# Differential scores of 128 rows, raw weight tiles by phase, and row sums behind the eighth up product

## The chip, the cores and the metric

The kernel runs on one core of a Trainium2 chip. The metric is the device time of one execution in microseconds (us). The engines are named as in the profile: PE is TensorE (PEld its weight loads), DVE is VectorE, ACT is ScalarE, POOL is GpSimd, and SP is SyncE, whose queue issues the DMAs. L12 is line 12 of the kernel.

## The reference

Two layers of a diffusion transformer block work on 512 tokens of 1024 channels: 256 latent tokens and 256 context tokens. In layer 1 only the latent tokens need an output. Cut to what matters here:

```
mod  = silu(c) @ w_mod[i] + b_mod[i]           # six vectors a layer; silu(c_ctx) for the context
h    = rms_norm(x) * (1 + mod[1]) + mod[0]
p    = split(h @ w_in[i])                      # q, k, v of four token mixers
# differential attention: 4 heads, 2 halves of 32 channels each
q, k = rope(rms_norm(q)), rope(rms_norm(k))    # context: no rope
sc   = (q @ k.T) / sqrt(32)                    # 8 score matrices
a    = softmax(sc[half 0]) - lam * softmax(sc[half 1])
yb   = a @ v
# neighbourhood (na), grouped (gq) and latent (ml) attention likewise
x    = x + mod[2] * (sum_i sigmoid(h @ w_gate[i]) * (y_i @ w_branch[i])) @ w_out
h2   = rms_norm(x) * (1 + mod[4]) + mod[3]
u    = conv3(h2 @ w_up)                        # 5632 channels, three taps along the tokens
x    = x + mod[5] * (silu(u_gate) * u_val) @ w_down
```

## The kernel before, in words

**Products.** Both factors of every large product are split into a high part, which TensorE's fp32r format holds, and the low rest, and three products are added up (hi hi, lo hi, hi lo): mm3, lines 277 to 280. Weights come in tiles of 128 x 1024 (512 KB). For each, wload (line 267) issues the DMA into a raw tile on SP's queue, ScalarE casts it to the high part wh (line 272), and VectorE subtracts to get the low part wl (line 257, in lo_of). The pools wraw, whi and wlo have four buffers each. Products accumulate in PSUM, in three buffers called acc; attention scores have two, sc, and transposes two, tp.

**Order.** The kernel is written with generators, drive() interleaves them by weights, and the framework's scheduler then fixes the order of each engine's queue. Each engine works its queue off in that order and waits by semaphores.

**Row sums.** The products with w_mod have a single row of input, so they are done on VectorE. mods (line 329) loads a raw tile of w_mod (line 339) and multiplies it, once for the latent and once for the context vector, with cact, silu of the conditioning laid out over all partitions, and sums along the row into one column of M (line 349). There are 128 such sums; 48 stand in the attention of layer 0 and its last merge, and the last 56 tiles of the plan (80 sums) are driven beside the MLP of layer 0 (line 1143) with four raw tiles of their own, the pool mr. cact (1 MB) is loaded near the start (line 945) and put through Silu on ScalarE (line 946).

**Differential scores.** use_qk normalizes and rotates queries and keys; to_ST (line 591) transposes them on TensorE (line 607) and takes the high and low parts from PSUM. head_scores (line 756) makes a score matrix of 128 queries and 512 keys (256 for the context's queries): one matmul of 64 rows (line 767: the high part against both parts of the other side) and one of 32 rows (line 768). In layer 1 neighbourhood and grouped attention are split like this too, with 64 channels: 128 rows and 64 rows.

**The MLP.** After the output projection (split_tail, line 1008, whose last three parts are worked off half by half so that the norm's sums of squares ss end early), each chunk of 128 channels is modulated (operations t and hl on VectorE, hh on ScalarE). ffn (line 1115) makes the first four up products of layer 0 in two halves of 256 tokens each, which are eight products of the generator, and from there 512 tokens at a time. conv (line 1066) puts the three taps onto each product: one operation on ScalarE, two on VectorE (u, lines 1075 and 1076), which free the acc buffer. Behind the 20th up product comes the first group of down products, down(0), which adds to xt. An up product of 512 tokens is 24 matmuls.

**The start of layer 1.** The loop at line 922 modulates a chunk for both halves of the tokens and multiplies it with the weights for keys and values of neighbourhood attention into four PSUM tiles kv, two for the latent and two for the context tokens (lines 929 to 932).

## Time and profile before

| what | us |
|---|---|
| time, median of 3 runs (lowest, highest) | 1481.22 (1481.22, 1482.71) |
| the profiled execution's own time | 1481.19 |
| its span, first to last instruction | 1479.4 |
| busy: PE / DVE / ACT / POOL | 1428.8 / 1054.5 / 667.5 / 204.3 |
| mean granted clock of TensorE | 0.989 |

The profile is of one execution. Busy times of an engine are those in which it works on an instruction; shares are of the span. A matmul's end is modelled, so the pace of TensorE is read from the distance between the starts of two matmuls and not from their durations, which overlap. "x4" behind a row joins four equal instructions. A releaser behind "<-" is the work whose end let a waiting instruction go.

### The profile page before, as it was taken

The page shows a single profiled execution, that of the slowest core. Times are in us where ns is not written, and L with a number is a line of the kernel's source. Part 1 is how long each engine was busy: PE and PEld are TensorE (multiplying, and loading weights), DVE is VectorE, ACT ScalarE, POOL GpSimd, SP SyncE. Part 2 cuts the span into 40 slices and gives each one's busy share as a digit, 9 for nine tenths or more (in the row PEclk, how much of TensorE's full clock was granted, in tenths as well). Part 3 has the DMA queues.
Part 4 walks back from the last instruction along what each step waited for, and adds up shares of the span by engine and source line. Part 5 has one row for each costly group of instructions (what it writes and reads, how often), then busy time and mean ns, then how long its engine had stood idle before and what let it go on. Part 6 is the DMA issues. An engine that isn't in the chain of part 4 may idle for free.

```text
span 1479.4 us, 22328 instructions
## 1 busy us (share of the span) xinstructions
PE 1428.8 (97%) x8526; PEld 1197.5 (81%) x8526; DVE 1054.5 (71%) x1911; ACT 667.5 (45%) x1197; POOL 204.3 (14%) x191
## 2 busy tenths in 40 slices
PE   6999999999999997999999999899999999899999
PEld 3787777776777887888888888798788889799999
DVE  5688676658776589999856553668777575787884
ACT  5445544444333333444134432356646544564662
POOL 0343001213111200000000000034122331000000
PEclk9999999999999998999999999999999999999999
DMA  9532122214234364568822322333232344455553
GB/s 377 189 103 77 45 88 68 83 53 133 86 114 165 135 218 152 193 221 272 282 94 92 99 93 79 107 101 121 72 104 93 115 140 132 132 182 184 180 179 113
DMA packets 57931, 202.19 MB, mean 137 GB/s; under 512 B 6561, under 2 KB 8097, under 8 KB 57185
## 3 DMA queue, kind: packets, MB, share of 16 engines
q1 hardware_dynamic: 57824, 200.77, 40.2%
q8 instruction: 67, 1.10, 0.3%
q14 instruction: 40, 0.32, 0.1%
HBM read 199.69 MB, written 1.05 MB: 136 GB/s over the span
## 4 chain that ended last, share of the span: by engine, by line
PE 88%; DVE 6%; issue 3%; ACT 2%; DMA 1%; POOL 0%; SPq 0%; POOLq 0%; DVEq 0%; ACTq 0%
PE acc L278 24%; PE acc L280 24%; PE acc L279 24%; PE av L834 3%; PE sc L753 3%; PE tp L826 2%; DVE junk L349 2%; PE sc L768 2%; PE sc L767 1%; DVE wl L257 1%; ACT wh L272 1%; DVE t L254 1%; DMA raw<-in_wb_dram 1%; DMA mraw<-in_wb_dram 1%; PE acc L729 1%
## 5 line engine op out<-in xcount | busy, mean ns | idle before, releaser
L272 ACT CAST wh<-raw 128x1024 fp32r<-128x1024 f32 (+1 forms) x272 | 279.8, 1029 | 438.2 <-PE acc L279 336.6
L257 DVE TENSOR_TENSOR wl<-raw,wh 128x1024 fp32r<-128x1024 f32 (+1 forms) x272 | 331.4, 1218 | 158.7 <-ACT wh L272 156.3
L278 PE MATMUL acc<-hh,wh 128*128 128x256 f32 (+1 forms) x1248 | 424.7, 342 | 15.8 <-DVE u L254 8.7
L279 PE MATMUL acc<-hl,wh 128*128 128x256 f32 (+1 forms) x1248 | 419.4, 337 | 0.8 <-DVE hl L254 0.8
L280 PE MATMUL acc<-hh,wl 128*128 128x256 f32 (+1 forms) x1248 | 420.1, 337 | 0.0
L278 PEld LDWEIGHTS acc<-hh,wh 128*128 128x128 f32 x1248 | 239.8, 193 | 44.5 <-issue 12.9
L279 PEld LDWEIGHTS acc<-hl,wh 128*128 128x128 f32 x1248 | 240.6, 193 | 26.6 <-issue 3.3
L280 PEld LDWEIGHTS acc<-hh,wl 128*128 128x128 f32 x1248 | 240.5, 193 | 26.5 <-issue 4.3
L257 POOL TENSOR_TENSOR r<-v,mhalf 128x4 f32<-128x4 f32 (+3 forms) x59 | 81.6, 1387 | 736.5 <-DVE v L404 461.8
L349 DVE SCALAR_TENSOR_TENSOR junk<-raw,cact 128x1024 bf16<-128x1024 f32 x128 | 156.8, 1225 | 21.7 <-DMA raw<-in_wb_dram 21.1
L278 PE MATMUL acc<-wh,hh 128*128 128x256 f32 (+3 forms) x496 | 148.8, 300 | 4.2 <-ACT hh L423 4.2
L279 PE MATMUL acc<-wl,hh 128*128 128x256 f32 (+3 forms) x496 | 147.5, 297 | 0.0
L280 PE MATMUL acc<-wh,hl 128*128 128x256 f32 (+3 forms) x496 | 145.1, 298 | 0.1
L279 PE MATMUL acc<-al,wh 128*128 128x256 f32 (+1 forms) x370 | 121.5, 328 | 0.0
L278 PE MATMUL acc<-ah,wh 128*128 128x256 f32 (+1 forms) x370 | 121.5, 328 | 0.0
L280 PE MATMUL acc<-ah,wl 128*128 128x256 f32 (+1 forms) x370 | 121.4, 328 | 0.0
L254 DVE SCALAR_TENSOR_TENSOR u<-acc,smt,u 128x255 f32<-128x255 f32 (+1 forms) x184 | 108.4, 593 | 1.5
L278 PEld LDWEIGHTS acc<-wh,hh 128*128 128x128 f32 x496 | 94.9, 191 | 14.1 <-ACT hh L423 7.1
L776 ACT ACTIVATE p<-sc,nm 128x512 f32<-128x512 f32 (+1 forms) x120 | 74.1, 618 | 66.0 <-DVE nm L773 37.9
L280 PEld LDWEIGHTS acc<-wh,hl 128*128 128x128 f32 x496 | 94.5, 191 | 9.4 <-issue 5.5
L279 PEld LDWEIGHTS acc<-wl,hh 128*128 128x128 f32 x496 | 95.0, 191 | 6.8 <-issue 4.6
L773 DVE TENSOR_REDUCE nm<-sc 128x1 f32<-128x512 f32 (+1 forms) x120 | 71.1, 597 | 35.4 <-PE sc L768 24.8
(165 smaller groups left out, 2067.7 us busy)
## 6 DMA issues: line engine op xcount, KB each, us to landing
raw<-in_wb_dram SPq DMA_DIRECT2D x328, 512.0 KB, 3.4
mraw<-in_wb_dram SPq DMA_DIRECT2D x16, 512.0 KB, 10.2
raw<-in_wb_dram SPq DMA_DIRECT2D x20, 384.0 KB, 2.9
x<-in_xT_dram SPq DMA_DIRECT2D x2, 1024.0 KB, 6.3
bt<-in_bias_dram SPq DMA_DIRECT2D x8, 256.0 KB, 3.2
xt<-in_xT_dram SPq DMA_DIRECT2D x2, 1024.0 KB, 7.1
raw<-in_wb_dram SPq DMA_DIRECT2D x4, 320.0 KB, 2.8
cact<-in_cb_dram SPq DMA_DIRECT2D x1, 1024.0 KB, 11.4
```

The source lines that it names most:

```text
L254: V.scalar_tensor_tensor(out=out, in0=in0, scalar=scalar, in1=in1, op0=op0, op1=op1)
L257: e.tensor_tensor(out=out, in0=a, in1=b, op=op)
L272: A.copy(h[:, :w], r[:, :w])
L278: mm(ps, lhsT=a[0], rhs=b[0], start=first, stop=False)
L279: mm(ps, lhsT=a[0], rhs=b[1], start=False, stop=False)
L280: mm(ps, lhsT=a[1], rhs=b[0], start=False, stop=last)
L349: V.scalar_tensor_tensor(out=junk, in0=r, scalar=1.0, in1=cact[:, st_], op0=ALU.mult, op1=ALU.mult, accum_out=o)
L753: mm(sps[:, :n], lhsT=q[o:o + d, c:c + P], rhs=k[o:o + d, T - n:], start=True, stop=True)
L768: mm(sps[:, :n], lhsT=q[r1, 4 + i, c:c + P], rhs=kk[r1], start=False, stop=True)
L773: V.tensor_reduce(out=nm, in_=sps[:, :n], op=ALU.max, axis=AX.X, negate=True)
L776: A.activation(out=p[:, :n], in_=sps[:, :n], func=AF.Exp, bias=nm, accum_out=s)
L834: mm(av[64 * j:64 * j + 64], lhsT=V_[:, 4 - nk + i, vcol(hd):vcol(hd) + 64], rhs=PTs[j][:, i], start=i == 0, stop=i == nk - 1, tile_positi ...
```

## The change

Five things are changed.

1. Raw weight tiles by phase: wraw has three buffers instead of four, and wraw_load takes its tile from a list of pools in turn. In the attention of layer 0 the list holds wraw alone. From the last merge of layer 0 to the end of its MLP, weights use wraw1 (four buffers), and the row sums use wraw; the pool mr is gone. In layer 1 the list is three times wraw and once wraw2 (one buffer).
2. cact moves into a pool that is opened only once the first layer's input tile is closed; its load and its Silu stand at the same place in the code, but wait for that space. The row sums' unused product goes into a temporary tile instead of the tile junk.
3. Differential queries and keys: to_D copies the high parts (ScalarE) and subtracts the low ones (VectorE) into a staging tile before the transposes, laid out so that each head's half fills 128 rows: hi, hi, lo, lo on one side and hi, lo, hi, lo on the other. One step later TensorE transposes it in four pieces and one operation brings it out of PSUM, on VectorE or ScalarE in turn. A score is then one matmul of 128 rows. The context's rows get their gain in a further multiplication on VectorE. The weight of this chain in drive goes from 12 + nq to 20 + nq.
4. The row sums beside the MLP are issued behind the last tap of the eighth product (tc.issue_after).
5. In layer 1 the loop at the start modulates the latent half of every chunk and serves the two latent kv tiles first, and then the context half with the other two.

```diff
-    wraw = pool("wraw", 4)
+    wraw = pool("wraw", 3)
...
+    cyc = [[wraw], 0]
+
     def wraw_load(l, key, n=1024):
-        r = wraw.tile([P, 1024], F32, name="raw")
+        cyc[1] += 1
+        r = cyc[0][cyc[1] % len(cyc[0])].tile([P, 1024], F32, name="raw")
         nc.sync.dma_start(out=r[:, :n], in_=wb[l, KIDX[key], :, :n])
...
-    cact = const.tile([P, 2, D], F32, name="cact")
-    junk = const.tile([P, D], mybir.dt.bfloat16, name="junk")
...
-                V.scalar_tensor_tensor(out=junk, in0=r, scalar=1.0, in1=cact[:, st_], op0=ALU.mult,
-                                       op1=ALU.mult, accum_out=o)
+                with tc.issue_after(behind) if behind is not None else nullcontext():
+                    V.scalar_tensor_tensor(out=tmp.tile([P, D], mybir.dt.bfloat16, name="t"), in0=r, scalar=1.0, in1=cact[:, st_], op0=ALU.mult,
+                                           op1=ALU.mult, accum_out=o)
...
+        def to_D(dst, src, i, isq):
...
+            def parts_():
+                w4 = stage().rearrange("p a n -> p (a n)").bitcast(F32R)
+                w = w4.rearrange("p (g x y d) -> p g x y d", g=4, x=2, y=2)
+                s = src.rearrange("p (g d) -> p g d", g=4).unsqueeze(2).to_broadcast([P, 4, 2, 32])
+                hi, lo = (w[:, :, 0], w[:, :, 1]) if isq else (w[:, :, :, 0], w[:, :, :, 1])
+                A.copy(hi, s)
+                tt(V, lo, s, hi.bitcast(F32), ALU.subtract)
+                got.append(w4.bitcast(F32))
+
+            def turn():
+                tp = tp_p.tile([P, 4, P], F32, name="tp")
+                for g in range(4):
+                    nc.tensor.transpose(tp[:, g], got[0][:, g * P:(g + 1) * P], ident)
+                evac(A if i else V, dst, tp)
+
+            return [parts_, turn]
...
+                elif key == "df":
+                    tt(V, v4(st, h), v4(st, h), dgt[:, tab].unsqueeze(1).unsqueeze(1).to_broadcast([P, na, h, d]), ALU.mult)
...
+                    fs = [to_D(z[:, 4 * i:4 * i + 4, a * P:(a + 1) * P], st[:, a, i * P:(i + 1) * P], i, dst is qT)
+                          for a in range(na) for i in range(2)]
...
+            if d == 32:
+                mm(sps[:, :n], lhsT=q[:, 4 * i + r, c:c + P], rhs=k[:, 4 * ik + r, T - n:], start=True, stop=True)
+                return sps, n
...
             for bc, p_ in zip(bcs, FULL):
-                modulate(xt, bc, s1, M, 0, c, p_)
+                if l == 0 or p_[2] == 0:
+                    modulate(xt, bc, s1, M, 0, c, p_)
...
+            for t in range(4) if l == 0 else range(2):
+                kv_mm(c, t)
+        if l:
+            for c in range(KD):
+                modulate(xt, bcs[1], s1, M, 0, c, FULL[1])
+                for t in range(2, 4):
+                    kv_mm(c, t)
...
+            ces = ExitStack()
+            cact = spool(ces, "cact", 1, side="right").tile([P, 2, D], F32, name="cact")
             nc.sync.dma_start(out=cact, in_=cb)
...
-                     win_block(l, "dq", qh, use_qk(qT, "df", 8, 32, *q32, vec("dgq"), 0, 1)), flush()), 12 + nq),
+                     win_block(l, "dq", qh, use_qk(qT, "df", 8, 32, *q32, vec("dgq"), 0, 1)), flush()), 20 + nq),
...
+            wes = ExitStack()
+            cyc[0] = [spool(wes, "wraw1", 4)]
...
-            stt(u3[:, :, 0:255], p3[:, :, 1:256], cw[:, 2:3], u3[:, :, 0:255], ALU.mult, ALU.add)
+            tap = stt(u3[:, :, 0:255], p3[:, :, 1:256], cw[:, 2:3], u3[:, :, 0:255], ALU.mult, ALU.add)
+            behind.append(tap.ins)
...
-            mrp = spool(fes, "mr", 4)
-            drive((body, 70), (mods(56, mrp, 2), 59))
+            with_order = mods(56, wraw, 2, behind[-1])
+            drive((body, 70), (with_order, 59))
...
+            cyc[0] = [wraw, wraw, wraw, ctx.enter_context(tc.tile_pool(name="wraw2", bufs=1))]
```

The order of VectorE's queue at the beginning of the MLP of layer 0, before, where the first chunks are modulated (t and hl); "junk,M<-raw,cact" is a row sum:

```order
L257 TENSOR_TENSOR wl<-raw,wh 128x1024
L254 SCALAR_TENSOR_TENSOR t<-xt,s_5389,sc 128x256 x2
L257 TENSOR_TENSOR ss<-ss,t 128x256
L349 SCALAR_TENSOR_TENSOR junk,M<-raw,cact 128x1024
L254 SCALAR_TENSOR_TENSOR hl<-t,M,hh 128x256
L254 SCALAR_TENSOR_TENSOR t<-xt,s_5389,sc 128x256
L254 SCALAR_TENSOR_TENSOR hl<-t,M,hh 128x256
L349 SCALAR_TENSOR_TENSOR junk,M<-raw,cact 128x1024
L404 TENSOR_SCALAR v<-tp 128x2
L254 SCALAR_TENSOR_TENSOR t<-xt,s_5389,sc 128x256 x2
```

The same place in the changed kernel:

```order
L257 TENSOR_TENSOR wl<-raw,wh 128x1024
L254 SCALAR_TENSOR_TENSOR t<-xt,s_5498,sc 128x256 x2
L257 TENSOR_TENSOR ss<-ss,t 128x256
L254 SCALAR_TENSOR_TENSOR hl<-t,M,hh 128x256
L254 SCALAR_TENSOR_TENSOR t<-xt,s_5498,sc 128x256
L254 SCALAR_TENSOR_TENSOR hl<-t,M,hh 128x256
L254 SCALAR_TENSOR_TENSOR t<-xt,s_5498,sc 128x256 x2
L254 SCALAR_TENSOR_TENSOR hl<-t,M,hh 128x256
L406 TENSOR_SCALAR v<-tp 128x2
L254 SCALAR_TENSOR_TENSOR hl<-t,M,hh 128x256
```

The row sums have left this part of the queue; from the first update of xt by the output projection to the eighth product's last tap there is none.

VectorE's queue among the up products of 512 tokens, before (u_...<-acc is a tap, wl the low part of a weight, al the low part of the activations):

```order
L257 TENSOR_TENSOR wl<-raw,wh 128x1024
L254 SCALAR_TENSOR_TENSOR u_5763<-acc,smt,u_5763 128x2x255
L349 SCALAR_TENSOR_TENSOR junk,M<-raw,cact 128x1024
L257 TENSOR_TENSOR al<-u_5572,ah 128x512
L254 SCALAR_TENSOR_TENSOR u_5763<-acc,smt,u_5763 128x2x255
L349 SCALAR_TENSOR_TENSOR junk,M<-raw,cact 128x1024
L257 TENSOR_TENSOR wl<-raw,wh 128x1024
L254 SCALAR_TENSOR_TENSOR u_5806<-acc,smt,u_5806 128x2x255
L349 SCALAR_TENSOR_TENSOR junk,M<-raw,cact 128x1024
L254 SCALAR_TENSOR_TENSOR u_5806<-acc,smt,u_5806 128x2x255
```

The changed kernel, directly behind the tap that ends the eighth product:

```order
L254 SCALAR_TENSOR_TENSOR u_5710<-acc,smt,u_5710 128x255 x2
L351 SCALAR_TENSOR_TENSOR t,M<-raw,cact 128x1024 x3
L257 TENSOR_TENSOR u_5681<-u_5681,u_5710 128x512
L351 SCALAR_TENSOR_TENSOR t,M<-raw,cact 128x1024 x2
L257 TENSOR_TENSOR wl<-raw,wh 128x1024
L254 SCALAR_TENSOR_TENSOR u_5869<-acc,smt,u_5869 128x2x255
L351 SCALAR_TENSOR_TENSOR t,M<-raw,cact 128x1024
L257 TENSOR_TENSOR al<-u_5681,ah 128x512
L351 SCALAR_TENSOR_TENSOR t,M<-raw,cact 128x1024 x2
L257 TENSOR_TENSOR wl<-raw,wh 128x1024
L254 SCALAR_TENSOR_TENSOR u_5869<-acc,smt,u_5869 128x2x255
L254 SCALAR_TENSOR_TENSOR u_5914<-acc,smt,u_5914 128x2x255
```

The sums stand there in threes. Counted over VectorE's queue, 72 of them lie between that tap and the last update of xt by down(0), and the other eight stand before the start of layer 1.

TensorE's queue at two differential scores of layer 0, before (L834 and L826 are products with the values and transposes of probabilities of an earlier score):

```order
L767 MATMUL sc<-kS,qS 128x512
L768 MATMUL sc<-kS,qS 128x512
L834 MATMUL av<-PT,Vt 64x256 x3
L826 MATMUL tp<-C,p 128x128 x4
L767 MATMUL sc<-kS,qS 128x512
L768 MATMUL sc<-kS,qS 128x512
```

The changed kernel (L646 is the transpose in to_D, L866 that of probabilities):

```order
L802 MATMUL sc<-kB,qB 128x512
L646 MATMUL tp<-C,st 128x128 x4
L866 MATMUL tp<-C,p 128x128 x2
L646 MATMUL tp<-C,st 128x128 x4
L802 MATMUL sc<-kB,qB 128x512
L646 MATMUL tp<-C,st 128x128 x4
```

Where two matmuls of part of the rows made a score, one stands now, and groups of four transposes have come in between.

## Rows read from the trace of the kernel before

**Rows 1.** The page, busy time by engine (us, share of the span, instructions) and the chain that ended last, by engine.

```profile
PE 1428.8 (97%) x8526; PEld 1197.5 (81%) x8526; DVE 1054.5 (71%) x1911; ACT 667.5 (45%) x1197; POOL 204.3 (14%) x191
...
PE 88%; DVE 6%; issue 3%; ACT 2%; DMA 1%; POOL 0%; SPq 0%; POOLq 0%; DVEq 0%; ACTq 0%
```

**Rows 2.** The table of stretches: from and to, length, busy us (and instructions) of PE, PEld, DVE, ACT and POOL, granted clock of TensorE, mean busy share of the DMA engines, GB/s.

```profile
20.00:40.00 20.00, 18.16 (x123) 11.53 (x123) 14.86 (x40) 13.09 (x21) 0.00 (x0) 1.00 1.02 411
60.00:260.00 200.00, 200.00 (x1147) 153.23 (x1146) 146.05 (x304) 97.46 (x209) 53.47 (x39) 1.00 0.24 76
520.00:608.00 88.00, 74.70 (x468) 69.30 (x467) 82.33 (x158) 32.14 (x55) 3.55 (x3) 0.92 0.57 191
960.00:1060.00 100.00, 99.62 (x671) 85.81 (x671) 76.98 (x142) 63.12 (x119) 34.70 (x26) 1.00 0.29 98
```

**Rows 3.** What TensorE waited for from 520 to 608 us: operation and line, releaser, us in total, times, longest.

```profile
PE acc L278 <- DVE u L254: 8.7, 2, 5.9
PE acc L278 <- ACT hh L423: 3.9, 1, 3.9
```

**Rows 4.** The timeline of TensorE from 588 to 596 us: start, duration, instruction; in brackets the idle time before it and its releaser.

```profile
588.91 0.55 PE L278 MATMUL acc<-hh,wh 128*128 128x256 f32 x1 [5.94 <-DVE u L254]
...
589.47 0.41 PE L280 MATMUL acc<-hh,wl 128*128 128x256 f32 x1
589.68 0.41 PE L278 MATMUL acc<-hh,wh 128*128 128x256 f32 x1
...
594.53 0.28 PE L280 MATMUL acc<-hh,wl 128*128 128x256 f32 x1
594.64 0.28 PE L278 MATMUL acc<-hh,wh 128*128 128x256 f32 x1
```

**Rows 5.** The timeline of VectorE from 596 to 601 us (same columns): two row sums with an operation between them, and a third directly behind the second.

```profile
596.83 1.22 DVE L349 SCALAR_TENSOR_TENSOR junk<-raw,cact 128x1024 bf16<-128x1024 f32 x1
...
597.98 0.48 DVE L254 SCALAR_TENSOR_TENSOR u<-acc,smt,u 128x255 f32<-128x255 f32 x1
598.37 1.21 DVE L349 SCALAR_TENSOR_TENSOR junk<-raw,cact 128x1024 bf16<-128x1024 f32 x1
...
599.63 1.23 DVE L349 SCALAR_TENSOR_TENSOR junk<-raw,cact 128x1024 bf16<-128x1024 f32 x1
```

**Rows 6.** The timeline of TensorE around 153 us: a differential score with 512 columns, and the matmuls behind it.

```profile
153.37 0.50 PE L767 MATMUL sc<-kS,qS 64*128 64x512 f32 x1
153.80 0.49 PE L768 MATMUL sc<-kS,qS 32*128 32x512 f32 x1
154.22 0.50 PE L279 MATMUL acc<-hl,wh 128*128 128x512 f32 x1
154.56 0.39 PE L280 MATMUL acc<-hh,wl 128*128 128x512 f32 x1
154.79 0.40 PE L278 MATMUL acc<-hh,wh 128*128 128x512 f32 x1
```

**Rows 7.** The same around 173 us: a differential score with 256 columns.

```profile
173.66 0.28 PE L280 MATMUL acc<-wh,hl 128*128 128x256 f32 x1
173.87 0.38 PE L767 MATMUL sc<-kS,qS 64*128 64x256 f32 x1
174.18 0.38 PE L768 MATMUL sc<-kS,qS 32*128 32x256 f32 x1
174.49 0.50 PE L278 MATMUL acc<-hh,wh 128*128 128x512 f32 x1
174.83 0.39 PE L279 MATMUL acc<-hl,wh 128*128 128x512 f32 x1
```

**Rows 8.** The same around 1001 us: the first matmuls of two scores of layer 1 that use all 128 rows (x2), and the one behind them.

```profile
1000.99 0.63 PE L767 MATMUL sc<-kS,qS 128*128 128x512 f32 x2
1001.46 0.28 PE L280 MATMUL acc<-wh,hl 128*128 128x256 f32 x1
```

**Rows 9.** Groups of TensorE's instructions by line and shape: rows of the array, output and type, count, busy us, mean ns of one, idle time before them. The second matmul of a score (L768, 32 rows) has the same counts as the first (L767, 64 rows).

```profile
L767 PE MATMUL sc<-kS,qS 64*128 64x512 f32 x32 | 15.9, 496 | 0.0
...
L607 PE MATMUL tp<-C,st 128*128 128x128 f32 x48 | 7.8, 274 | 0.0
...
L767 PE MATMUL sc<-kS,qS 64*128 64x256 f32 x16 | 6.1, 381 | 0.0
```

**Rows 10.** The timeline of TensorE around 1010 us: two groups of four transposes.

```profile
1009.83 0.60 PE L826 MATMUL tp<-C,p 128*128 128x128 f32 x4
1010.27 0.60 PE L607 MATMUL tp<-C,st 128*128 128x128 f32 x4
```

**Rows 11.** The table of stretches again, from the ninth up product to the end of the first group of down products.

```profile
605.80:740.00 134.20, 134.15 (x602) 111.44 (x603) 126.16 (x204) 49.31 (x63) 0.00 (x0) 1.00 0.75 250
```

**Rows 12.** Groups of VectorE's instructions by line and shape in that stretch: count, busy us, mean ns of one, idle time before them.

```profile
L349 DVE SCALAR_TENSOR_TENSOR junk<-raw,cact 128x1024 bf16<-128x1024 f32 x48 | 58.4, 1218 | 0.9 <-DMA raw<-in_wb_dram 0.8
```

**Rows 13.** The page, the row sums over the whole span.

```profile
L349 DVE SCALAR_TENSOR_TENSOR junk<-raw,cact 128x1024 bf16<-128x1024 f32 x128 | 156.8, 1225 | 21.7 <-DMA raw<-in_wb_dram 21.1
```

**Rows 14.** The page, the DMA issue of cact (count, KB, us to landing).

```profile
cact<-in_cb_dram SPq DMA_DIRECT2D x1, 1024.0 KB, 11.4
```

**Rows 15.** The timeline of ScalarE around 29 us: the operation on cact.

```profile
29.36 1.91 ACT L946 ACTIVATE cact<-cact 128x2048 f32<-128x2048 f32 x1
```

**Rows 16.** The timeline of TensorE at the start of layer 1.

```profile
951.40 0.60 PE L402 MATMUL tp<-C,ss 128*128 128x1 f32 x4 [3.31 <-DVE ss L257]
```

More of the change, by code (lines that the diff above doesn't have):

```diff
@@ L1 @@
-from contextlib import ExitStack
+from contextlib import ExitStack, nullcontext
 import math
@@ L253, in stt @@
     def stt(out, in0, scalar, in1, op0, op1):
-        V.scalar_tensor_tensor(out=out, in0=in0, scalar=scalar, in1=in1, op0=op0, op1=op1)
+        return V.scalar_tensor_tensor(out=out, in0=in0, scalar=scalar, in1=in1, op0=op0, op1=op1)
     def tt(e, out, a, b, op):
@@ L327, in backbone, with mods @@
             for c in range(KD)]
-    def mods(n, raws, ahead=0):
+    def mods(n, raws, ahead=0, behind=None):
         todo = [plan.pop(0) for _ in range(n)]
@@ L541, in backbone @@
         split = SPLIT[l]
-        nbig = 2 if "na" in split else 1
         def newkq(key):
-            if nbig == 1 and key in ("na", "gq"):
-                kT[key] = qp.tile([P, 2, T], F32, name="kT", bufs=1)
-                qT[key] = qp.tile([P, 2, TT], F32, name="qT", bufs=1)
-            else:
-                kT[key] = qp.tile([P, 4, T], F32, name="kS", bufs=nbig)
-                qT[key] = qp.tile([P, 6, TT], F32, name="qS", bufs=nbig)
+            if key in split and key != "df":
+                kT[key] = qp.tile([P, 4, T], F32, name="kA", bufs=1)
+                qT[key] = qp.tile([P, 6, TT], F32, name="qA", bufs=1)
+            elif key in ("na", "gq"):
+                kT[key] = qp.tile([P, 2, T], F32, name="kA", bufs=1)
+                qT[key] = qp.tile([P, 2, TT], F32, name="qA", bufs=1)
+            else:
+                kT[key] = qp.tile([P, 8, T], F32, name="kB", bufs=1)
+                qT[key] = qp.tile([P, 8, TT], F32, name="qB", bufs=1)
             if key in split:
@@ L621, in to_ST @@
                     stt(lo, tp[rs], g, hi[rs].bitcast(F32), ALU.mult, ALU.subtract)
+        def to_D(dst, src, i, isq):
+            got = []
+            def parts_():
[12 more added lines that the diff above has]
+            return [parts_, turn]
         def cols(j):
@@ L647, in f @@
                     st, g = s2, None
+                elif key == "df":
+                    tt(V, v4(st, h), v4(st, h), dgt[:, tab].unsqueeze(1).unsqueeze(1).to_broadcast([P, na, h, d]), ALU.mult)
                 z = dst[key][:, :, tcols(t0, na)]
+                if key == "df":
+                    fs = [to_D(z[:, 4 * i:4 * i + 4, a * P:(a + 1) * P], st[:, a, i * P:(i + 1) * P], i, dst is qT)
+                          for a in range(na) for i in range(2)]
+                    steps = [fs[0][0]]
+                    for x, y_ in zip(fs, fs[1:]):
+                        steps.append(lambda x=x, y_=y_: (y_[0](), x[1]()))
+                    return steps + [fs[-1][1]]
                 def put():
@@ L918, in backbone, with kv_mm @@
         kv = [(acc_p if t < 3 else av_p).tile([P, 512], F32, name="acc" if t < 3 else "av") for t in range(4)]
-        w = None
+        w = []
+        def kv_mm(c, t):
+            mm3(kv[t], tuple(z[:, c, t * P:(t + 1) * P] for z in (hh, hl)), tuple(z[:, c % 2] for z in w[c // 2]),
+                c == 0, c == KD - 1)
         for c in range(KD):
@@ L926, in backbone @@
             for bc, p_ in zip(bcs, FULL):
-                modulate(xt, bc, s1, M, 0, c, p_)
+                if l == 0 or p_[2] == 0:
+                    modulate(xt, bc, s1, M, 0, c, p_)
             if c % 2 == 0:
-                w = wload(l, ("nakv", c // 2), 2, 512)
-            for t in range(4):
-                mm3(kv[t], tuple(z[:, c, t * P:(t + 1) * P] for z in (hh, hl)), tuple(z[:, c % 2] for z in w),
-                    c == 0, c == KD - 1)
+                w.append(wload(l, ("nakv", c // 2), 2, 512))
+            for t in range(4) if l == 0 else range(2):
[5 more added lines that the diff above has]
+                    kv_mm(c, t)
         rt = lay.tile([P, 2, 2, 2, RW], F32, name="rt", bufs=1)
@@ L936, in backbone @@
         nc.sync.dma_start(out=rgt, in_=rg[l].rearrange("p (a w) -> p a w", a=4))
+        dgt = lay.tile([P, 2, 32], F32, name="dgt")
+        A.copy(dgt, rgt.rearrange("p (j s) w -> p j s w", s=2)[:, :, 0, 64:96])
         rtab0 = tmp.tile([P, 2, 2, RW], F32, name="t")
@@ L1058, in backbone @@
         us = {}
+        behind = []
         def up_ps(ff, w_, a, b):
@@ L1148, in backbone @@
             bcs = accs["bc"]
+            wes.close()
+            ces.close()
+            cyc[0] = [wraw, wraw, wraw, ctx.enter_context(tc.tile_pool(name="wraw2", bufs=1))]
 _ORDER = ["wb", "xT", "cc", "cb", "sm", "rg", "bias", "cst"]
```

## The prediction

> **What bounds the kernel now.** I read the page's shares first: TensorE is busy for 97% of the span and makes 88% of the chain that ended last, VectorE 6% [rows 1]. So a microsecond taken from TensorE's queue is a microsecond of the result wherever TensorE has no gap, and work on another engine matters only where TensorE waits for it. The second view is the table of stretches [rows 2]: from 60 to 260 us TensorE is busy for 200.00 of 200 us and from 960 to 1060 for 99.62 of 100. These two hold most of the differential scores. The exception is 520 to 608 us, where the output projection ends and the gated MLP of layer 0 begins: TensorE 74.70 of 88 us at a granted clock of 0.92, VectorE 82.33. The third view is what TensorE waited for there [rows 3]: two waits for the convolution's tap (u, 8.7 us), one for the modulated input (hh, 3.9 us). Each long one is followed by matmuls at the lower of the two clock levels: 0.21 us from one 256-column matmul to the next instead of 0.12 [rows 4]. In that stretch VectorE's queue has row sums between all other work; one takes 1.14 us of the queue before another operation and 1.26 before another sum [rows 5].
>
> **Scores of 128 rows.** A pair of today (64 rows, then 32) costs far more than its columns. With 512 columns the two start 0.43 us apart and the next matmul 0.42 us later; that one is left after 0.34 us where the one after it is left after 0.23 [rows 6], so 0.11 us more goes on the way out; the way in costs 0.09 us (0.21 us where 0.12 is usual) [rows 7]. Together 0.43 + 0.42 + 0.11 + 0.09 = 1.05 us. With 256 columns it is 0.31 + 0.31 + 0.11 + 0.09 = 0.82 us [rows 7]. A score that uses all 128 rows stands in the trace too: two of them take 0.47 us, 0.235 each, and nothing is lost behind them [rows 8]. There are 32 pairs of the wide and 16 of the narrow form [rows 9]: 32 x (1.05 - 0.235) + 16 x (0.82 - 0.12) = 26.1 + 11.2 = 37.3 us less.
>
> The cost is transposes. Each of seven calls that turn differential queries or keys issues 16 instead of 4 (48 transposes stand in the table now, those of all keys and queries [rows 9]): 84 more, 21 groups of four at 0.44 us [rows 10], 9.2 us. ScalarE and VectorE make about as many splits as before and two evacuations each more a call, beside a busy TensorE: hidden, and some 0.6 us a call where they are not. Net 28.1 us less; I keep one group's 0.44 us per call for a wait in the chain copy, subtract, transpose: -25 us. Bounds: -28, and -9.5 if the 128-row form keeps the starts of 0.42 and 0.31 us (32 x 0.43 + 16 x 0.31 - 9.2).
>
> What the rows show is that a matmul on part of the rows costs more than one on all of them, and that its neighbours pay too. The Trainium skill, "TensorEngine Tiling (Array Packing)", section "Key Properties", says why: changing the tiling mode drains the engine. By that the whole 37 us go, and the trace agrees (0.42 us against 0.235). The rule that speaks against the change is in "TensorE: Matmul & The Clock Gate", section "Why this matters for your kernels": a single matmul of few rows takes as long as one of 128. The 0.42 us against 0.235 contradicts it here; it is weighed as a rival below.
>
> **No sums ahead of the eighth up product.** Of the waits in [rows 3] the two for the tap (8.7 us) are waits behind a VectorE queue in which a sum follows every two or three operations; in the new order no sum stands between the output projection's first update of xt and the eighth tap. Without them a chunk's modulation costs VectorE about 0.8 us (two operations of 256 columns at 0.39 us, as the one of that size in [rows 5]), less than the 1.08 us that TensorE takes for its 9 matmuls of 0.12 (the first three products go through the chunks side by side). With the 5.9 us wait the low clock behind it goes too: from 588.9 to 594.4 us, some 5.5 us at little over half pace, 2.4 us. 8.7 + 2.4 = 11 us less. The 3.9 us wait is a chain of single steps (sum of squares, its root, first modulation) and I let it stand. Bounds: -18 if it and its slow matmuls go as well, -4 if the taps, which still stand behind modulations, keep TensorE waiting.
>
> **All sums behind it.** This is where I expect most of the gain to be given back. From 605.8 to 740 us, the other 16 up products and the first group of down products, TensorE is busy for all but 0.05 of 134.2 us and VectorE for 126.2 [rows 11], 48 sums among it [rows 12]. In the new order 72 of the 80 sums of this layer's MLP stand between the eighth tap and the last update of xt by that group, three at a time. 24 more at 1.22 us are 29.3 us: VectorE has 155.5 us of work where TensorE has 134.2, 21.3 us too much. The queue is in order, so the taps that free TensorE's three accumulators and the low halves of the weights stand behind sums, and TensorE falls back to VectorE's pace. It can work two products ahead of a late tap (24 matmuls of 0.227 us [rows 6], 5.45 us each), which may hide up to 10.9 us; against that, handing over at every product costs something. I take +20. Bounds: 0, if TensorE's lead and the 8 us in which VectorE idles now hide all, and +43, if in addition the waits for tiles that the sums show in the whole span, 21.1 us in all [rows 13], fall here.
>
> **The start.** The 1 MB of cact leaves the first loads: it takes 11.4 us to land [rows 14] between tiles that TensorE waits for, and the DMA engines are full at that time (share 1.02 from 20 to 40 us [rows 2]); at the 411 GB/s of that row it is 2.5 us of transfer, and its 1.91 us on ScalarE goes from the modulation's path [rows 15]. I take -3; bounds -5 and +4, since the first sums now wait for the later cact and hold what is queued behind them.
>
> **Layer 1's start.** TensorE waits 3.31 us for the last sum of squares [rows 16]. The new loop needs half the modulations before all four key and value tiles have to be served, but eight sums move in front of this place. -1.5; bounds -4 and +3. The pools (three instead of four raw tiles at times) cost nothing while the weights land 3 us after issue, against 5.45 us a product.
>
> **Sum.** The profiled execution took 1481.19 us around its span of 1479.4, the median of the three runs is 1481.22, so either serves. -25 - 11 + 20 - 3 - 1.5 = -20.5: 1461 us.
>
> **Rivals.**
> *Sums decide* (slower). A sum may start only when its 512 KB tile has landed, the tile's buffer (one of three) is free only when an older sum is done, and VectorE waits in order: waits of this kind make 21.1 us of today's span [rows 13]. With three sums in a row on three buffers, each group can meet one. From 24 groups, 1 us each gives +24 on top of the +20: 1485 us. It decides from 41 us lost in that stretch, where the other terms' gain of 40.5 is used up. Against it: in today's stretch with 48 sums VectorE waits for a tile for 0.9 us only [rows 12].
> *Sums hidden.* The lead of accumulators and weights covers the excess and the term is 0: 1441 us. For it speaks that TensorE loses nothing now with VectorE at 126 of 134 us; against it, the 155.5 us.
> *Scores half as good.* The new score keeps the long starts, or TensorE waits for the longer chain of splits: -9.5 instead of -25, 1476 us.
> *Few rows cost nothing.* If a score's second matmul costs only its columns, the change saves 32 x 0.227 + 16 x 0.12 = 9.2 us and spends 9.2 on transposes; the term is 0 and the time 1486 us. [Rows 6 to 8] speak against it. The Trainium skill's rule named above is this one.
>
> **How the numbers follow.** Forecast 62%, sums decide 14%, sums hidden 9%, scores half as good 11%, few rows cost nothing 4%. About 0.2%, 3 us, is what a measurement of this kernel can tell from no change. The forecast ends faster in 58 of its 62, half scores in 8 of 11, hidden sums always; no change takes 3 of the forecast, 3 of half scores, 3 of the sums' rival and 1 of the last; the rest is slower: 75, 10 and 15%. The range for 8 in 10 is 1443 to 1484 us: below, all of the scores and an excess mostly hidden (-28 - 11 + 5 - 3 - 1.5 = -38.5); above, an excess near the rival's point.
>
> **What would show it.** One score matmul with 0.235 us to its successor, and no longer starts around it. Between the output projection and the ninth up product no wait for u of over 1 us. Behind the eighth tap, VectorE without a gap for over 140 us and TensorE with waits for u or wl that add to about 20 us, spread over the 16 products. I am wrong if TensorE has no gap there, if sums wait for DMA in it, or if the stretches of the differential scores shrink by less than 20 us.

## The result, and the profile after

The changed kernel takes 1488.29 us (median of 11 runs, 1486.41 to 1493.8) against 1481.41 us before (11 runs): a ratio of 1.0054, 95% interval 1.0040 to 1.0067. It is 6.9 us slower by the medians; 1461 us was forecast. The profiled execution has a span of 1485.7 us.

The page of the changed kernel, engines and chain (as [rows 1]):

```profile
PE 1414.7 (95%) x8562; PEld 1199.1 (81%) x8562; DVE 1053.5 (71%) x1928; ACT 659.1 (44%) x1201; POOL 207.1 (14%) x191
...
PE 83%; DVE 8%; issue 3%; ACT 2%; DMA 2%; POOL 1%; SPq 0%; POOLq 0%; DVEq 0%; ACTq 0%
```

TensorE has 14.1 us less to do than before, and the span is 6.3 us longer all the same: 20 us of new idle time. TensorE's share of the chain falls from 88 to 83%. To find the places I took marks from the timeline of TensorE: the second matmul of the output projection of layer 0 (the first with a low part), the first up product of 512 columns (the ninth product), the first up product behind down(0), the last matmul of layer 0, and the second of the output projection of layer 1. In us from mark to mark:

| kernel | to projection 0 | to ninth product | to end of down(0) | to end of layer 0 | to projection 1 | to the last matmul |
|---|---|---|---|---|---|---|
| before | 520.4 | 88.6 | 130.7 | 207.7 | 303.2 | 225.1 |
| changed | 516.2 | 74.1 | 154.7 | 207.7 | 304.9 | 224.5 |
| forecast of the difference | -20 | -11 | +20 | 0 | -9.5 | 0 |
| difference | -4.2 | -14.5 | +24.0 | 0 | +1.7 | -0.6 |

(The forecast's -25 for the scores is split here as their counts are, 17 in layer 0 and 8 in layer 1.) The MLP of layer 0 came out as forecast, +9.5 us for +9. The two attentions, with the start and the loop in them, did not: of the 29.5 us less expected there, 2.5 came.

**The up products.** What TensorE waited for from 560 to 620 us and from 620 to 750 us (two answers; columns as in [rows 3]). In the first stretch the waits for u are nearly gone:

```profile
PE acc L281 <- ACT hh L425: 2.8, 1, 2.8
PE acc L281 <- DVE u L254: 2.1, 3, 1.0
```

```profile
PE acc L281 <- DVE u L254: 13.5, 4, 6.7
PE acc L281 <- DVE M L257: 1.6, 1, 1.6
```

In the second they are back, with 13.5 us. The stretches behind the eighth tap (columns as in [rows 2]):

```profile
600.00:620.00 20.00, 18.15 (x79) 14.44 (x78) 20.00 (x31) 6.52 (x9) 0.00 (x0) 1.00 0.67 227
620.00:640.00 20.00, 12.74 (x53) 9.91 (x52) 20.00 (x32) 6.38 (x9) 0.00 (x0) 0.92 0.64 213
640.00:660.00 20.00, 18.40 (x74) 14.75 (x73) 20.00 (x33) 6.70 (x9) 0.00 (x0) 0.91 0.60 194
660.00:680.00 20.00, 15.93 (x69) 12.51 (x68) 20.00 (x34) 6.07 (x8) 0.00 (x0) 1.00 0.63 207
680.00:700.00 20.00, 17.80 (x66) 14.53 (x67) 19.85 (x33) 5.88 (x8) 0.00 (x0) 0.83 0.77 262
```

VectorE is busy for 99.85 of 100 us, TensorE for 83.02, where [rows 11] had it busy throughout. The third column from the right tells a second cost: granted clocks of 0.92, 0.91 and 0.83, from two stretches of 6.8 us at the low level, each of which begins towards the end of a wait of over 6 us. The timeline of VectorE ahead of the longest wait (TensorE goes on at 638.42):

```profile
632.97 1.21 DVE L351 SCALAR_TENSOR_TENSOR t<-raw,cact 128x1024 bf16<-128x1024 f32 x1
634.11 0.08 DVE L351 DVE_READ_ACCUMULATOR t<-raw,cact 128x1 f32 x1
634.11 1.22 DVE L351 SCALAR_TENSOR_TENSOR t<-raw,cact 128x1024 bf16<-128x1024 f32 x1
635.25 0.08 DVE L351 DVE_READ_ACCUMULATOR t<-raw,cact 128x1 f32 x1
635.25 1.22 DVE L351 SCALAR_TENSOR_TENSOR t<-raw,cact 128x1024 bf16<-128x1024 f32 x1
636.40 0.08 DVE L351 DVE_READ_ACCUMULATOR t<-raw,cact 128x1 f32 x1
636.40 1.22 DVE L257 TENSOR_TENSOR wl<-raw,wh 128x1024 fp32r<-128x1024 f32 x1
637.53 0.74 DVE L254 SCALAR_TENSOR_TENSOR u<-acc,smt,u 128x510 f32<-128x510 f32 x1
```

Three sums and the low half of a weight stand in front of the tap whose end frees an accumulator. No sum waits for a DMA here. Sums directly behind each other start 1.14 us apart now, where two stood 1.26 us apart before [rows 5].

**The scores.** A new score among other matmuls (timeline of TensorE; compare [rows 6] and [rows 7]):

```profile
175.35 0.40 PE L802 MATMUL sc<-kB,qB 128*128 128x512 f32 x1
175.59 0.39 PE L282 MATMUL acc<-hl,wh 128*128 128x512 f32 x1
...
181.37 0.28 PE L802 MATMUL sc<-kB,qB 128*128 128x256 f32 x1
181.49 0.39 PE L281 MATMUL acc<-hh,wh 128*128 128x512 f32 x1
```

It takes 0.24 us with 512 columns and 0.12 with 256, and its neighbours keep their pace, as forecast. But not all stand like that. Another place, and what all transposes waited for (the second fence is the grouping by line and shape):

```profile
158.53 0.63 PE L646 MATMUL tp<-C,st 128*128 128x128 f32 x4 [1.54 <-DVE st L257]
...
159.92 0.66 PE L646 MATMUL tp<-C,st 128*128 128x128 f32 x4 [0.55 <-ACT PT L588]
...
162.71 0.63 PE L646 MATMUL tp<-C,st 128*128 128x128 f32 x4 [1.02 <-DVE qB L592]
```

```profile
L646 PE MATMUL tp<-C,st 128*128 128x128 f32 x112 | 18.5, 293 | 6.6 <-DVE st L257 4.9 <-DVE qB L592 1.0 <-ACT PT L588 0.5
```

The transposes kept TensorE waiting for 6.6 us, 4.9 of them for the split on VectorE; one wait, of 2.70 us at 1035.64, has 6.8 us of low clock behind it.

**A wait that no step had.** In the last merge of layer 0:

```profile
459.12 0.79 PE L281 MATMUL acc<-hh,wh 128*128 128x512 f32 x1 [4.69 <-ACT wh L275]
```

TensorE waits for a weight, and from 455.9 to 462.7 us the granted clock is at the low level (columns as in [rows 2]):

```profile
455.90:462.73 6.83, 3.61 (x9) 2.84 (x10) 4.75 (x4) 4.18 (x4) 0.00 (x0) 0.50 1.02 420
```

The DMA issues on SP's queue ahead of it, and what that queue waited for longest from 430 to 465 us (us in total, times, longest):

```profile
417.67 0.33 SPq L267 DMA_DIRECT2D raw<-in_wb_dram  x1
424.80 26.85 SPq L340 DMA_DIRECT2D raw<-in_wb_dram  x4
451.70 2.22 SPq L267 DMA_DIRECT2D raw<-in_wb_dram  x4
```

```profile
SPq L340 <- DVE rs L818: 20.2, 2, 13.5
```

Line 267 loads weights, line 340 the tiles of the row sums. From 417.67 to 451.70 us no weight was issued; then four come at once, one for each buffer of wraw1, the pool that the change opens there. A tile by itself lands some 3 us after its issue; these four landed after 4.7 to 7.4 us, so most of the delay came ahead of the transfer. What ended the pause can be read off: the last of the four row sum tiles waited 13.5 us for VectorE to free its buffer, and the first weight went out 0.05 us behind it with no wait of its own in the trace. Since when the space of wraw1 had been free, the trace does not tell.

### The profile page after: what moved, and what is told of

It is laid out like the page before. It is cut to its first block, busy times and chain, and to the rows that moved or that the text cites. A ratio compares the mean times of both kernels' runs of the same rounds, so it can differ in the third digit from the quotient of the medians.

```text
span 1485.7 us, 22425 instructions
## 1 busy us (share of the span) xinstructions
PE 1414.7 (95%) x8562; PEld 1199.1 (81%) x8562; DVE 1053.5 (71%) x1928; ACT 659.1 (44%) x1201; POOL 207.1 (14%) x191
## 4 chain that ended last, share of the span: by engine, by line
PE 83%; DVE 8%; issue 3%; ACT 2%; DMA 2%; POOL 1%; SPq 0%; POOLq 0%; DVEq 0%; ACTq 0%
PE acc L281 24%; PE acc L282 23%; PE acc L283 23%; PE av L874 3%; PE sc L790 3%; DVE t L351 3%; PE tp L866 2%; DVE wl L257 2%; DVE u L254 1%; ACT wh L275 1%; PE tp L646 1%; DMA raw<-in_wb_dram 1%; PE tp L373 1%; POOL st L257 1%; DMA mraw<-in_wb_dram 1%
## 5 line engine op out<-in xcount | busy, mean ns | idle before, releaser
L351 DVE SCALAR_TENSOR_TENSOR t<-raw,cact 128x1024 bf16<-128x1024 f32 x128 | 153.9, 1226 | 7.8 <-POOL y L257 4.7
L816 ACT ACTIVATE p<-sc,nm 128x512 f32<-128x512 f32 (+1 forms) x120 | 74.1, 619 | 55.2 <-DVE nm L813 35.4
```

The lines of the kernel that those rows point to most:

```text
L351: V.scalar_tensor_tensor(out=tmp.tile([P, D], mybir.dt.bfloat16, name="t"), in0=r, scalar=1.0, in1=cact[:, st_], op0=ALU.mult, op1=ALU.mul ...
L816: A.activation(out=p[:, :n], in_=sps[:, :n], func=AF.Exp, bias=nm, accum_out=s)
```

## Experiments

All times are medians; the ratios are to runs of the kernel before on the same chip (its medians: 1483.27 us for experiments 1 to 4, 1482.87 for 5 to 8, 1482.1 for 9 to 12, 1482.54 for 13 to 15).

**1. Three tiles from the old pool.**

```diff
-            cyc[0] = [spool(wes, "wraw1", 4)]
+            cyc[:] = [[wraw] * 3 + [spool(wes, "wraw1", 4)] * 200, -1]
```

> The changed kernel, but the first three weight tiles from the last merge of layer 0 on are taken from the pool wraw, which is there all along, and only the fourth and later ones from wraw1, which is opened at that point. Theory 1 (the pool that opens late costs TensorE the 4.69 us wait for wh at 459 us and the 6.8 us at the low clock behind it): that wait falls below 1 us and no low clock follows it before 480 us; 6 to 8 us less, about 1481 us. Rival (the wait is VectorE's or the DMA engines', whichever pool): the wait stays and the time is 1488 within 2 us.

1480.69 us, ratio 0.9982 (0.9973 to 0.9992). The issues in the same stretch:

```profile
417.61 0.33 SPq L267 DMA_DIRECT2D raw<-in_wb_dram  x1
424.81 0.33 SPq L340 DMA_DIRECT2D raw<-in_wb_dram  x1
431.82 5.91 SPq L267 DMA_DIRECT2D raw<-in_wb_dram  x2
439.69 0.33 SPq L340 DMA_DIRECT2D raw<-in_wb_dram  x1
443.83 0.33 SPq L267 DMA_DIRECT2D raw<-in_wb_dram  x1
```

Weights flow again, the wait and the low clock behind it are gone, and the projection starts at 510.0 instead of 516.2 us. Against before the ratio falls by 0.72%, some 11 us; between the two profiled executions it is 7.3 us of span. So these first loads cost 7 to 11 us, alone enough to turn the result from slower into a little faster. The edit changes which space the first tiles use and also SP's order; which of the two made the loss is not told apart.

**2. Sums without the rule.**

```diff
-            with_order = mods(56, wraw, 2, behind[-1])
+            with_order = mods(56, wraw, 2)
```

> The changed kernel without the rule that the MLP's row sums are issued behind the eighth product; the scheduler places them (21 fall between products 1 and 4, 46 between products 4 and 20). Theory 1 (the sums behind the eighth product cost about 20 us there and save about 11 ahead of it, so the rule costs 9): TensorE's waits for u between 600 and 750 us shrink from 17 us to under 8, waits for u ahead of the ninth product come back with 4 to 9 us, and the time falls by 4 to 10 us, to about 1481. Rival (the rule gains, and the loss of the whole is elsewhere): slower by 3 us or more.

1494.31 us, ratio 1.0073 (1.0056 to 1.0090): slower by some 3 us than the changed kernel (the intervals overlap), against the first theory and at the edge of the rival's. TensorE's waits from 563 to 720 us:

```profile
PE acc L281 <- DVE u L254: 19.0, 8, 6.1
PE acc L281 <- ACT hh L425: 2.8, 1, 2.8
PE acc L281 <- DVE M L257: 1.7, 2, 1.3
```

The scheduler does not go back to the order of before, where sums were drawn into the output projection: it puts 21 ahead of the ninth product's first tap, where they hurt again (82.9 us to the ninth product), and the rest behind it, still 150.8 us to the end of down(0). Taking the rule away is not the same as undoing the change.

**3. Sums spread over the MLP.**

```diff
-                with tc.issue_after(behind) if behind is not None else nullcontext():
+                with tc.issue_after(behind[-1]) if behind is not None else nullcontext():
...
-            with_order = mods(56, wraw, 2, behind[-1])
+            with_order = mods(56, wraw, 2, behind)
```

> The changed kernel with each row sum issued behind the last tap that the program has written at that point, not behind the eighth product's: 46 sums fall between the fifth product and the end of the first down group and the other 34 later, where VectorE idles. Theory 1 (sums are dear only where VectorE has no spare time): no wait for u over 1.5 us and no low clock between 600 and 750 us, 16 to 22 us less, about 1470 us. Rival (the waits for u come from taps standing behind modulations and from accumulators, not from the sums' number): less than 6 us gained.

1464.92 us, ratio 0.9875 (0.9856 to 0.9893). From 560 to 720 us TensorE waits for u for 0.2 us:

```profile
PE acc L281 <- ACT hh L425: 2.8, 1, 2.8
PE acc L281 <- DVE u L254: 0.2, 1, 0.2
```

The ninth product begins after 74.1 us as in the changed kernel, and down(0) ends 130.6 us later instead of 154.7. The sums themselves cost nothing where VectorE has time; 72 of 80 in one stretch cost 24 us.

**4. The old scores in the changed kernel.** newkq, use_qk and head_scores are those of before.

```diff
...
-            if d == 32:
-                mm(sps[:, :n], lhsT=q[:, 4 * i + r, c:c + P], rhs=k[:, 4 * ik + r, T - n:], start=True, stop=True)
-                return sps, n
...
-                     win_block(l, "dq", qh, use_qk(qT, "df", 8, 32, *q32, vec("dgq"), 0, 1)), flush()), 20 + nq),
+                     win_block(l, "dq", qh, use_qk(qT, "df", 8, 32, *q32, vec("dgq"), 0, 1)), flush()), 12 + nq),
```

> The changed kernel with the differential scores of before: to_ST, a matmul of 64 rows and one of 32, the chain's weight 12 + nq. All else as changed. Theory 1 (the scores save about 25 us of TensorE's queue in all, but a third or more comes back as waits for the split tiles and low clock behind one): 8 to 18 us slower than the changed kernel, about 1500 us, with no wait of a transpose for a split of over 1 us at the start of layer 1. Rival (what the scores save is all lost again): within 3 us of 1488.

1501.95 us, ratio 1.0123 (1.0101 to 1.0144): 13.7 us slower than the changed kernel by the medians, 10 by the ratios. The scores are a gain, of half the size forecast. The marks give 8.8 us in layer 0's attention and 3.0 in layer 1's. With the scores the edit puts back the buffers of the key and query tiles (in layer 1 two of one kind, where the change has one each of two kinds) and the chain's weight; the three are measured together.

**5. Both gains together.** Experiments 1 and 3 in one kernel.

> Both edits that gained, together: row sums each behind the newest tap, and the first three weight tiles of the last merge from wraw. Theory 1 (two separate places, 24 us of accumulators and weights held up behind sums, 7.6 us of a pool that opens late): the gains add up, about 1457 us, with no wait of TensorE over 3 us between 440 and 930 us. Rival (one hides the other): 1462 or more.

1455.71 us, ratio 0.9815 (0.9801 to 0.9829): they add up. This is the fastest kernel here that does all of the work, 27 us less than before.

**6. The split two steps ahead** (on 5).

```diff
-                    steps = [fs[0][0]]
-                    for x, y_ in zip(fs, fs[1:]):
-                        steps.append(lambda x=x, y_=y_: (y_[0](), x[1]()))
-                    return steps + [fs[-1][1]]
+                    steps = [fs[0][0], fs[1][0]]
+                    for x, y_ in zip(fs, fs[2:]):
+                        steps.append(lambda x=x, y_=y_: (x[1](), y_[0]()))
+                    return steps + [f_[1] for f_ in fs[-2:]]
```

> As spread_first3, and the split tiles of differential queries and keys are made two steps ahead of their transposes instead of one. Theory 1 (part of what the scores lose is waits of the transposes for the split, 2.1 to 2.7 us with 6.8 us of low clock behind it at the start of layer 1, about 3 us in layer 0): 4 to 8 us less than spread_first3 and no wait of L646 for st of over 1 us. Rival (the wait only moves to the next step, since VectorE is late by more than a step): within 2 us of spread_first3.

1457.41 us, ratio 0.9825 (0.9809 to 0.9842): no gain. The wait of the transposes in layer 1 is still 2.08 us (2.19 in 5), others moved. More lead in the program's text did not bring the split earlier here.

**7. The old loop at the start of layer 1** (on 5): both halves modulated, four tiles served at once.

```diff
-                if l == 0 or p_[2] == 0:
+                if True:
...
-            for t in range(4) if l == 0 else range(2):
+            for t in range(4):
...
-        if l:
+        if False:
```

> As spread_first3, but the loop at the start of layer 1 is that of before (both halves of a chunk modulated, four kv tiles served at once). If the new loop costs (theory: the changed kernel takes 304.9 us from the end of layer 0 to the output projection of layer 1 and 307.9 with the old scores, where before took 303.2, and the loop is what differs): 2 to 5 us less than spread_first3. Rival (the loop gains 1.5 us, as forecast): 1 to 4 us more.

1459.14 us, ratio 0.9842 (0.9827 to 0.9856): the new loop gains about 3.5 us, a little more than the 1.5 forecast.

**8. The kernel before with spread sums alone** (as 3; the last tap of each product is put into behind as in the change).

```diff
-                V.scalar_tensor_tensor(out=junk, in0=r, scalar=1.0, in1=cact[:, st_], op0=ALU.mult,
-                                       op1=ALU.mult, accum_out=o)
+                with tc.issue_after(behind[-1]) if behind is not None else nullcontext():
+                    V.scalar_tensor_tensor(out=junk, in0=r, scalar=1.0, in1=cact[:, st_], op0=ALU.mult,
+                                           op1=ALU.mult, accum_out=o)
...
-            drive((body, 70), (mods(56, mrp, 2), 59))
+            drive((body, 70), (mods(56, mrp, 2, behind), 59))
```

> The kernel before with one change alone: the MLP's row sums of layer 0 are each issued behind the newest tap of the up products. Theory 1 (today's stalls ahead of the ninth product, 14.5 us with the low clock, come from sums in VectorE's queue, and spread sums cost nothing later): 12 to 17 us faster than before, about 1468 us. Rival (the stalls are those of the modulation itself, and the gain in the changed kernel came from the scores or the pools): under 6 us faster.

1468.71 us, ratio 0.9903 (0.9889 to 0.9918): 14 us less. From the projection to the ninth product it takes 76.2 us: 12.4 of the changed kernel's 14.5 us come with the sums alone.

**9. The old scores in 5.** The edit of 4.

> As spread_first3, but with the differential scores of before (to_ST, matmuls of 64 and 32 rows, chain weight 12 + nq): what the scores are worth where no sum and no pool holds TensorE up. Theory 1 (the pairs, with what they cost their neighbours, are worth 37 us of TensorE as forecast 28 with transposes, but the trace of the changed kernel shows 14.9 us from start to start for the new scores instead of 9.4 and 12.5 instead of 9.2 for the transposes, and waits besides): 10 to 16 us slower than spread_first3, about 1469 us. Rival (the 25 us of the forecast were there and something else of the changed kernel ate them): 20 us slower or more.

1468.75 us, ratio 0.9910 (0.9893 to 0.9928): against 0.9815 that is 14 us (13 by the medians). Without the other two losses, too, the scores are worth 13 to 14 us, not 25.

**10. Half of the transposes** (on 5). to_D leaves out two of its four transposes and brings the other two out twice.

```diff
-                for g in range(4):
+                for g in range(2):
                     nc.tensor.transpose(tp[:, g], got[0][:, g * P:(g + 1) * P], ident)
-                evac(A if i else V, dst, tp)
+                evac(A if i else V, dst.rearrange("p (a b) t -> p a b t", a=2),
+                     tp[:, :2].unsqueeze(1).to_broadcast([P, 2, 2, P]))
```

> As spread_first3, but to_D makes two of its four transposes and brings the two pieces out twice, in one operation of the same size: 56 transposes fewer, and half of the scores' operands are wrong. If the transposes cost their 0.11 us each and no more: 6 us less than spread_first3. If they cost more by where they stand (array switches, waits): 8 us or more less. If they stand in TensorE's gaps: under 3 us.

1455.28 us, ratio 0.9814 (0.9797 to 0.9831): 56 matmuls less and nothing gained. The mean granted clocks of 5 and of this one:

```profile
core 0: 1452.0 us, clock 0.992
```

```profile
core 0: 1454.3 us, clock 0.985
```

TensorE waits for the split all the same (5.4 us instead of 4.1), and the profile has stretches at the low level at 142, 159, 559 and 1094 us that 5 does not have: TensorE is busy for 35.8 us at the low level instead of 17.2. Half of the difference, an estimated 9 us, would account for the lost gain in this pair of executions. But it is the slowest of the five of 10 (1456.05 us) against the fastest of the five of 5 (1453.76). Over all of them the mean granted clock is 0.985 to 0.992 (median 0.989) here and 0.989 to 0.992 (0.991) in 5, and at 0.992 each 10 took 1451.69 us, 2 us less than 5. The stretch at 559 us stands behind a wait of 2.76 us for hh that 5 has too (2.77 us), without low clock. So the clock is a part of the answer at most; that the chain through VectorE and ScalarE is the bound at these places is not shown.

**11 and 12. The chain's weight** (on 5): 12 + nq, and 30 + nq.

```diff
-                     win_block(l, "dq", qh, use_qk(qT, "df", 8, 32, *q32, vec("dgq"), 0, 1)), flush()), 20 + nq),
+                     win_block(l, "dq", qh, use_qk(qT, "df", 8, 32, *q32, vec("dgq"), 0, 1)), flush()), 12 + nq),
```

> As spread_first3, with the chain of the differential queries and keys at the weight 12 + nq that it had before instead of 20 + nq, so that the program writes more of the chain's steps early. If the waits of the transposes for the split come from the chain being written too late: 2 to 5 us less. If the weight fits the longer chain (20 steps instead of 12): within 2 us or slower.

> As spread_chain_12 with 30 + nq: the same question from the other side; a large weight writes the chain's steps closer together and earlier against the attention's. Expected by the theory that the scheduler's placing decides and not the weight: within 3 us of spread_first3, as spread_chain_12.

1461.91 us, ratio 0.9866 (0.9851 to 0.9881), and 1467.35 us, ratio 0.9904 (0.9888 to 0.9919): 7.5 and 13 us slower. For 12 the second reading came, that 20 fits the longer chain; for 30 the expectation that the weight matters little was wrong. The weight alone, which changes only the order in which the work is written, moves the time by more than experiments 6, 7, 13 and 14 do. With 30 the transposes come far ahead of their split (waits from 1000 to 1040 us):

```profile
PE tp L646 <- DVE st L257: 8.8, 2, 8.5
PE sc L807 <- ACT p L816: 1.6, 1, 1.6
```

**13. Sums done before layer 1** (on 5).

```diff
-            drive((body, 70), (with_order, 59))
+            drive((body, 70), (with_order, 80))
```

> As spread_first3, with the row sums driven at the weight 80 instead of 59, so that only two instead of 16 stand behind the last up product, and none in front of layer 1. Theory A (the sums at the start of layer 1 and the loads of their tiles delay layer 1): from the end of layer 0 to the output projection 300 us or less instead of 304, 3 to 5 us less in all. Theory B (they fall into VectorE's spare time): within 2 us of spread_first3.

1455.84 us, ratio 0.9821 (0.9805 to 0.9838): the same. Layer 1 reaches its projection after 301.7 us instead of 304.0, between the two theories, but layer 0 takes 6.7 us longer in the profiled execution, the slowest of its four (1459.57 us). The time shows no gain.

**14. The new loop in 8.** The part of the change's diff on kv_mm and modulate, in 8.

> before_spread with the new loop at the start of layer 1 and nothing else. If the loop gains by itself, as it did among the other changes (3.4 us): 1465 us and about 299 us from the end of layer 0 to the output projection. If it is the loop that costs layer 1 its 2 to 5 us here: 1470 or more.

1466.35 us, ratio 0.9890 (0.9877 to 0.9904): 2 us less than 8, with overlapping intervals; 300.4 us instead of 302.3 to layer 1's projection agrees. So the loop seems a gain by itself too.

**15. Old scores and old loop in 5.** The edits of 4 and 7.

> As spread_first3, with the old scores and the old loop: left of the change are the pools of raw tiles, the place of cact and the sums, here spread. If the pools cost layer 1 the rest: 307 us or more from the end of layer 0 to the output projection where before_spread has 302.3, and about 1472 us in all against 1468.7. If the pools cost nothing: 302 to 304 us there.

1469.32 us, ratio 0.9914 (0.9900 to 0.9928), with 305.8 us in layer 1 to its projection where 8 has 302.3: between the two expectations. The projection of layer 0 starts at 518.0 us where it did at 522.3 in 8. So the pools and the place of cact gain some 4 us in layer 0 and seem to give about 3.5 back in layer 1. Of these 3.5, however, an estimated 2.4 are the clock: at the start of layer 1 TensorE is busy for 8.15 us at the low level here and for 3.41 in 8, and half of the difference is lost. That the pools hold layer 1 up is not shown.

## Why the prediction was wrong

**The failed steps** are two. "The pools ... cost nothing while the weights land 3 us after issue, against 5.45 us a product" answers the wrong question: the issue came 34 us after the one before it. I had the three buffers in mind and not the first loads of wraw1, which in the changed kernel stand on SP's queue behind four row sum tiles that wait for VectorE, and which cannot go out before the attention's space is free. Which of the two held them longer is open; together they are 7 to 11 us (experiment 1), and no rival had them.

The second is a size: the scores' -25 us measured -10 to -14 (4 and 9), near the weak end of its bounds. The sign and the price of a pair held; so did the sign that the prediction gave for being wrong here, stretches of scores that shrink by less than 20 us (8.8 and 3.0). From the starts of all matmuls: the 96 old matmuls of the pairs took 37.5 us of the queue and the neighbours 8.6, as the forecast had it. The 48 new ones took 14.9 us instead of 9.4, since in places a score is followed by a wait or by a matmul of another kind, and the transposes 12.5 more instead of 9.2. That leaves 18.7 of the 28.1 us. Of the rest, 4.9 us are waits for the split that the chain copy, subtract, transpose brought, with low clock behind the longest; I kept 3 us for them. That clock had no term in the sum: behind this wait TensorE is busy for 6.1 us at the low level, by an estimate half of it lost, 3 us more. The rival "scores half as good" named this outcome; its other cause, long starts, did not occur among full matmuls (8 of the 48 took that long, most of them beside a product with the values or a wait).

**What held.** No sums ahead of the ninth product: -14.5 us for -11, and experiment 8 shows the sums as the cause of 12.4 of them. (The matmul at 605.8 us was the first of the eighth product, not the ninth, which starts at 608.94; both kernels are compared at the ninth here.) All sums behind it: +24.0 us for +20, VectorE with hardly a gap until 723 us, and experiment 3 takes it away by spreading them. Of my two rivals on that term neither came: sums waited for their tiles for 3.1 us in all, nearly all of it behind 723 us, where TensorE had no gap, and TensorE's lead hid little. That the sizes agree is in part luck. TensorE's waits were 17.0 us, not spread over the 16 products but 12.7 of them in two waits of over 6 us, and none ended later than 682.2 us. The part I had left out is the clock: the stretch at the low level at each of the two waits costs an estimated 5.5 us together (TensorE is busy for 11.0 us in them). The start: TensorE is busy for 45.70 of the first 60 us instead of 42.63, -3.1 us for -3; with the old scores and the old loop (experiment 15) it is 45.52, so this comes with cact's place and the pools, which were not tried apart. The loop: -2 to -3.5 us for -1.5, and about 3.5 us against it in layer 1, most of it clock in one pair of executions.

**The sum by the runs:** scores -12, ahead of the ninth product -14.5, behind it +24, pool +9, start -3, loop -2.7, layer 1 without scores and loop +3.5: +4.3 us. Measured are 6.9 us, by the ratio's interval 6 to 10; 2 to 6 us are not accounted for.

The weighed rule of the Trainium skill, that a single matmul of few rows takes as long as one of 128 ("TensorE: Matmul & The Clock Gate", section "Why this matters for your kernels"), does not hold for the pairs as they stand in this queue: 0.43 us a matmul [rows 6] against 0.24 for one of 128 rows with the same 512 columns.

## What to carry to other kernels

When a pool is split into phases, look in SP's queue at the first loads of the new phase and at what stands in front of them: here none went out for 34 us, though a tile lands in 3. Work that VectorE can do at any time cost 24 us here in one heap and nothing when each piece was tied to the newest product, so count it stage by stage against the spare time, not over the span. And do not count on all that is taken from a busy TensorE: two thirds of the matmul time saved here, and half of the forecast, arrived.

## What was not expected of the hardware

56 transposes fewer left the time where it was (1455.28 against 1455.71 us). The granted clock has a part in it that can't be put to a number: one and the same kernel was granted 0.985 to 0.992 in its five executions, and they took 1456.05 to 1451.69 us.

The same wait is not always followed by low clock. In the changed kernel a wait of 2.70 us (at 1035.64) has a stretch of 6.8 us at the low level at its end, and one of 1.54 us (at 158.53) has none. A wait of 1.54 us stands at this place in the profiles of experiments 1, 2, 3, 5, 7 and 13 too: low level follows in 1 (3.4 us), 2 (3.4 us) and 13 (6.8 us), and none in 3, 5 and 7. So a low stretch in one profile is not yet an effect of the edit.
